# Down projection in halves of 1024 columns, five of 22 pairs of k-tiles by Strassen's seven products

## The chip, the cores and the metric

The kernel runs on one core of a Trainium2 chip. The metric is the device time of one execution in microseconds (us), the median of several runs. The engines have short names in the rows: PE is TensorE's matmul, PEld its load of a stationary operand, DVE is VectorE, ACT is ScalarE, POOL is GpSimd, SP is SyncE, whose queue carries most of the transfers.

## What is computed

One decoder block on 256 tokens (two blocks of 128, called b = 0 and 1) with a model width of 2048:

```python
h = rms_norm(x, w_norm_mix);  proj = h @ w_in          # attention and mLSTM heads follow
x = x + concat([attn_out, mlstm_out]) @ w_out
h2 = rms_norm(x, w_norm_ffn)
x = x + (silu(h2 @ w_ffn_gate) * (h2 @ w_ffn_up)) @ w_ffn_down     # 2048 -> 5632 -> 2048
gate = sigmoid(rms_norm(x, w_norm_ple) @ w_ple_gate)
e = rms_norm(p @ w_ple_proj, w_ple_post_norm)
return x + gate * e
```

All data is float32. The change is in the feed-forward part and its borders: `w_ffn_gate`, `w_ffn_up` and, above all, `w_ffn_down`.

## The kernel before

**How float32 is multiplied.** Each operand is split into a high part rounded to fp32r (a cast on ACT, line 220 for weights) and the rest (a subtraction on DVE, line 221). A product is three matmuls of 128x128 by 128x512: high by high, high by rest, rest by high. `load_piece` (line 212) brings two k-tiles of 512 weight columns (512 KB) into a tile `wr`; `halves` makes `wh` and `wl` of it. `wr`, `wh` and `wl` have four buffers each. A buffer comes free when its last reader is done: `wr` after DVE's subtraction, `wh` and `wl` after the last matmul that reads them.

**The gate and up projection** (`gate_up`, matmuls in lines 742 to 744) runs over eleven chunks of 512 columns. The 16 k-tiles of h2 are taken in eight pairs. A plain pair (`plain_unit`) is two k-tiles by two token blocks by two weights, that is eight products, 24 matmuls. For the pairs 1 and 2 `seven_unit` treats tokens by k-tiles, and k-tiles by (gate, up), as 2 by 2 blocks and takes Strassen's form (Winograd's variant) with seven products, P1 to P7, 21 matmuls. It needs combinations of the weights (tiles `wt`: `t12` and `t34`, four subtractions or additions on DVE in lines 702 to 706, then their halves) and of the tokens (`make_forms`, lines 667 to 678, once per pair: tiles `fh`, `fl`). P1, P5, P6 and P7 have four banks of PSUM of their own, and after the last such pair their sums are formed (lines 749 to 755: `t1`, `qr`, `su`) and later added to the other four banks (lines 757 to 760). A chunk's order is 0, 3, 1, 4, 5, 2, 6, 7 (first chunk: 0, 3, 4, 1, 5, 2, 6, 7): 6 x 24 + 2 x 21 = 186 matmuls.

**The down projection** is `residual(..., "ple")`: four chunks of 512 columns, each one call of `linear` over all 44 k-tiles, 44 x 2 x 3 = 264 matmuls (lines 262 to 264), then two additions to `xres` (line 636) and the task `after`, which transposes the new columns for the next projection: over DRAM by POOL's queue (`split_by_blocks`, lines 187 to 196), and for the last chunk on PE (line 165).

**After it** `e_chunks` multiplies p by `w_ple_proj` (48 matmuls), ACT copies the results out (line 817), and the gate projection runs with 16 pieces of weights per column chunk.

**What sets the order.** Small pieces of work are generators in a list (`Task`); `advance` lets them step between the units of a projection. The tool chain then orders each engine's instructions again by a plan of its own, so that the order on an engine is not that of the code. Engines execute in that order and wait on semaphores.

## Time and profile before

| | |
|---|---|
| median of 3 runs | 1221.85 us (1220.7 to 1222.06) |
| the profiled execution's own time | 1227.3 us |
| its span, from first to last instruction | 1225.1 us |
| PE, DVE, ACT busy in the span | 99%, 70%, 51% |
| mean granted clock of PE | 0.998 of full speed |

The profile is of one execution, which took 5.45 us more than the median. 2.2 us of its time lie outside the span. A busy share counts an instruction from start to end; matmuls overlap each other, so the distance from one start to the next says what a matmul costs, and a wait of a few tenths of a us between two matmuls does not show as idle time.

### The profile page before, as it was taken

The page shows a single profiled execution, that of the slowest core. Times are in us where ns is not written, and L with a number is a line of the kernel's source. Part 1 is how long each engine was busy: PE and PEld are TensorE (multiplying, and loading weights), DVE is VectorE, ACT ScalarE, POOL GpSimd, SP SyncE. Part 2 cuts the span into 40 slices and gives each one's busy share as a digit, 9 for nine tenths or more (in the row PEclk, how much of TensorE's full clock was granted, in tenths as well). Part 3 has the DMA queues.
Part 4 walks back from the last instruction along what each step waited for, and adds up shares of the span by engine and source line. Part 5 has one row for each costly group of instructions (what it writes and reads, how often), then busy time and mean ns, then how long its engine had stood idle before and what let it go on. Part 6 is the DMA issues. An engine that isn't in the chain of part 4 may idle for free. (4 is left out here: it accounts for less than half of the span.)

```text
span 1225.1 us, 15485 instructions
## 1 busy us (share of the span) xinstructions
PE 1211.5 (99%) x5609; PEld 1003.9 (82%) x5609; DVE 854.3 (70%) x1188; ACT 622.8 (51%) x823; POOL 79.5 (6%) x149
## 2 busy tenths in 40 slices
PE   9999999999999999999999999999999999999998
PEld 6899978878888787888788888878888888888888
DVE  5766755565565898888879889888855554545754
ACT  6555556545555545555544555554544444446542
POOL 1111000000011000000000000000000000000000
PEclk9999999999999999999999999999999999999999
DMA  7677744575678667676676776667676666665762
GB/s 262 213 233 221 236 138 131 173 227 157 202 239 254 192 204 232 219 217 210 209 253 194 234 219 216 222 208 251 201 262 206 212 210 210 208 206 170 232 227 92
DMA packets 136384, 257.33 MB, mean 210 GB/s; under 512 B 10002, under 2 KB 29300, under 8 KB 136308
## 3 DMA queue, kind: packets, MB, share of 16 engines
q1 hardware_dynamic: 127156, 229.06, 59.2%
q0 software_dynamic: 8400, 26.22, 6.6%
q8 instruction: 44, 0.72, 0.2%
q10 hardware_dynamic: 752, 1.06, 0.2%
q14 instruction: 32, 0.26, 0.1%
HBM read 241.10 MB, written 15.20 MB: 209 GB/s over the span
## 5 line engine op out<-in xcount | busy, mean ns | idle before, releaser
L221 DVE TENSOR_TENSOR wl<-wr,wh 128x1024 fp32r<-128x1024 f32 (+2 forms) x445 | 508.6, 1154 | 289.4 <-ACT wh L220 288.5
L220 ACT CAST wh<-wr 128x1024 fp32r<-128x1024 f32 (+2 forms) x445 | 439.0, 997 | 449.2 <-PE acc L264 259.1
L262 PE MATMUL acc<-wh,act_h 128*128 128x512 f32 (+2 forms) x864 | 320.6, 371 | 0.1
L263 PE MATMUL acc<-wl,act_h 128*128 128x512 f32 (+2 forms) x864 | 318.0, 368 | 1.6 <-DVE wl L221 1.6
L264 PE MATMUL acc<-wh,act_l 128*128 128x512 f32 (+2 forms) x864 | 317.8, 368 | 0.0
L263 PEld LDWEIGHTS acc<-wl,act_h 128*128 128x128 f32 x864 | 163.0, 189 | 25.8 <-DVE wl L221 2.9
L262 PEld LDWEIGHTS acc<-wh,act_h 128*128 128x128 f32 x864 | 163.1, 189 | 24.6 <-ACT act_h L133 0.9
L264 PEld LDWEIGHTS acc<-wh,act_l 128*128 128x128 f32 x864 | 162.8, 188 | 24.5 <-DVE act_l L135 0.6
L191 POOL DMA_DIRECT2D swap<-tq x100 | 61.0, 616 | 882.1 <-DVE tq L187 882.1
L743 PE MATMUL acc<-wl,act_h 128*128 128x512 f32 x272 | 107.0, 393 | 0.1
L744 PE MATMUL acc<-wh,act_l 128*128 128x512 f32 x272 | 106.0, 390 | 0.0
L742 PE MATMUL acc<-wh,act_h 128*128 128x512 f32 x272 | 103.7, 390 | 0.0
L263 PE MATMUL acc<-wl,gh 128*128 128x512 f32 x224 | 88.3, 394 | 0.0
L262 PE MATMUL acc<-wh,gh 128*128 128x512 f32 x224 | 87.8, 392 | 0.0
L264 PE MATMUL acc<-wh,gl 128*128 128x512 f32 x224 | 86.9, 388 | 0.0
L220 ACT CAST wh<-wt 128x1024 fp32r<-128x1024 f32 x44 | 46.2, 1050 | 55.4 <-DVE wt L703 54.4
L742 PE MATMUL tr<-wh,act_h 128*128 128x512 f32 x178 | 69.5, 391 | 0.2 <-ACT wh L220 0.2
L743 PE MATMUL tr<-wl,act_h 128*128 128x512 f32 x178 | 69.7, 392 | 0.0
L744 PE MATMUL tr<-wh,act_l 128*128 128x512 f32 x178 | 69.3, 389 | 0.0
L743 PEld LDWEIGHTS acc<-wl,act_h 128*128 128x128 f32 x272 | 51.0, 188 | 13.7 <-DVE wl L221 3.3
L742 PEld LDWEIGHTS acc<-wh,act_h 128*128 128x128 f32 x272 | 51.1, 188 | 11.0
L744 PEld LDWEIGHTS acc<-wh,act_l 128*128 128x128 f32 x272 | 51.1, 188 | 10.4
(259 smaller groups left out, 1328.2 us busy)
## 6 DMA issues: line engine op xcount, KB each, us to landing
wr<-in_w_ffn_gate_dram SPq DMA_DIRECT2D x88, 512.0 KB, 3.5
wr<-in_w_ffn_up_dram SPq DMA_DIRECT2D x88, 512.0 KB, 4.5
wr<-in_w_ffn_down_dram SPq DMA_DIRECT2D x88, 512.0 KB, 4.6
wr<-in_w_in_dram SPq DMA_DIRECT2D x63, 512.0 KB, 4.7
wr<-in_w_in_dram SPq DMA_DIRECT2D x48, 344.0 KB, 3.7
wr<-in_w_out_dram SPq DMA_DIRECT2D x32, 512.0 KB, 4.3
wr<-in_w_ple_gate_dram SPq DMA_DIRECT2D x32, 512.0 KB, 4.6
swap<-tq POOLq DMA_DIRECT2D x100, 128.0 KB, 3.6
```

Source lines behind the costliest of these rows:

```text
L191: nc.gpsimd.dma_start(out=d[:, :, :, i, :].rearrange("j c b e -> c b j e"), in_=t[32 * i:32 * i + 32].rearrange("c b j k r -> c b j (k r)"))
L220: nc.scalar.copy(wh, wr)
L221: nc.vector.tensor_tensor(wl, wr, wh.bitcast(F32), op=ALU.subtract)
L262: nc.tensor.matmul(po[b][:, 0:n], ah[:, kk, s], wh[:, j, :], start=count == 1, stop=False)
L263: nc.tensor.matmul(po[b][:, 0:n], ah[:, kk, s], wl[:, j, :], start=False, stop=False)
L264: nc.tensor.matmul(po[b][:, 0:n], al[:, kk, s], wh[:, j, :], start=False, stop=count == total)
L742: nc.tensor.matmul(bank[n], lh, rh, start=first, stop=False)
L743: nc.tensor.matmul(bank[n], lh, rl, start=False, stop=False)
L744: nc.tensor.matmul(bank[n], ll, rh, start=False, stop=left[n] == 0)
```

## The change

The down projection runs in two halves of 1024 columns. In each half the 22 pairs of k-tiles go by a written order; the pairs 8, 10, 12, 14 and 16 take the seven products, with the two blocks of 512 columns in the place of gate and up. A half uses all eight banks of PSUM, so that its sums and additions come once for 1024 columns. The four seven-product sums are added to `xres` apart from the other four banks.

In the gate and up projection `seven_unit` makes the halves in another order and takes P2 as second product, the sums are written in the code behind the halves of the unit that follows, and the sigmoid's tile is `qr` instead of a tile of its own. Around them: columns 1024 to 1535 are transposed on PE too (`after` with c == 2); p is loaded by POOL's queue instead of SP's; the weight row of the last norm is loaded in two transfers of 1024 columns instead of four of 512; `sq` has one buffer instead of two; `rows_b` lies in another pool; `after_up` steps with a gap of 3.

```diff
     def sumsq(dst, src):
-        sq = small.tile([P, 512], BF16, name="sq")
+        sq = small.tile([P, 512], BF16, name="sq", bufs=1)
...
-                if c == 3 and name == "ple":
+                if c >= 2 and name == "ple":
...
                 if c == 3:
+                    while not made_by[id(nxt[2][0])].done:
+                        yield held
...
-                po = linear(w, acts, c * 512, 512, pieces=pieces, width=1 if pieces else 2)
-                for b in range(2):
-                    nc.vector.tensor_tensor(xres[:, b, cs], po[b], xres[:, b, cs], op=ALU.add)
+                if half is None:
+                    po = linear(w, acts, c * 512, 512)
+                    for b in range(2):
+                        nc.vector.tensor_tensor(xres[:, b, cs], po[b], xres[:, b, cs], op=ALU.add)
+                elif c % 2 == 0:
+                    half(c // 2)
...
         def after_up(dst, gg):
-            yield from split_by_blocks(dst, lambda b: gg[b])
+            yield from split_by_blocks(dst, lambda b: gg[b], gap=3)
...
             ra, rb = (load_piece(w, 2 * p, 2, c * 512, 512) for w in (w_gate, w_up))
+            ah, al = halves(ra)
             t12 = fp.tile([P, 2, 512], F32, name="wt", bufs=2)
             nc.vector.tensor_tensor(t12[:, 0], ra[:, 0], rb[:, 0], op=ALU.subtract)
             nc.vector.tensor_tensor(t12[:, 1], t12[:, 0], rb[:, 1], op=ALU.add)
+            h12, l12 = halves(t12)
             t34 = fp.tile([P, 2, 512], F32, name="wt", bufs=2)
             nc.vector.tensor_tensor(t34[:, 0], t12[:, 1], ra[:, 0], op=ALU.subtract)
             nc.vector.tensor_tensor(t34[:, 1], ra[:, 1], t12[:, 1], op=ALU.subtract)
-            ah, al = halves(ra)
-            h12, l12 = halves(t12)
+            h34, l34 = halves(t34)
             bh, bl = halves(rb[:, 1:2])
-            h34, l34 = halves(t34)
-            right = {"P1": (ah[:, 0], al[:, 0]), "P6": (h12[:, 1], l12[:, 1]), "P5": (h12[:, 0], l12[:, 0]),
-                     "P2": (ah[:, 1], al[:, 1]), "P7": (h34[:, 0], l34[:, 0]), "P4": (h34[:, 1], l34[:, 1]),
+            right = {"P1": (ah[:, 0], al[:, 0]), "P2": (ah[:, 1], al[:, 1]), "P6": (h12[:, 1], l12[:, 1]),
+                     "P5": (h12[:, 0], l12[:, 0]), "P7": (h34[:, 0], l34[:, 0]), "P4": (h34[:, 1], l34[:, 1]),
                      "P3": (bh[:, 0], bl[:, 0])}
...
+                if su is None and left["P1"] == 0:
+                    while held:
+                        advance(1)
+                    t1 = fp.tile([P, 512], F32, name="t1")
+                    nc.scalar.copy(t1, bank["P1"])
+                    qr = quads.tile([P, 2, 512], F32, name="quad")
+                    nc.vector.tensor_tensor(qr[:, 0], bank["P6"], t1, op=ALU.add)
+                    nc.vector.tensor_tensor(qr[:, 1], bank["P7"], qr[:, 0], op=ALU.add)
+                    su = quads.tile([P, 2, 512], F32, name="tq")
+                    for i in range(2):
+                        nc.vector.tensor_tensor(su[:, i], bank["P5"], qr[:, i], op=ALU.add)
                 for n, (lh, ll), (rh, rl) in unit:
...
                     nc.tensor.matmul(bank[n], ll, rh, start=False, stop=left[n] == 0)
-                if su is None and left["P1"] == 0:
...
-                sg = fp.tile([P, 512], F32, name="sg", bufs=2)
+                sg = qr[:, b]
...
-        def load_p():
-            yield
-            yield
-            p_sb = fp.tile([P, 512], F32, name="gg0").rearrange("p (b k) -> p b k", b=2)
-            nc.sync.dma_start(out=p_sb, in_=p.rearrange("(b p) k -> p b k", p=P))
-            for _ in range(6):
-                yield
-            yield from transpose_in(acts_p, lambda b, j: p_sb[:, b, j * P:(j + 1) * P], 0, 2)
-        made_by[id(acts_p[0])] = Task(load_p())
...
-                wpost = fp.tile([P, 512], F32, name="sg", bufs=2)
-                nc.sync.dma_start(out=wpost, in_=w_ple_post[0, cs].partition_broadcast(P))
+                if c % 2 == 0:
+                    wpost = fp.tile([P, 1024], F32, name="wt", bufs=2)
+                    nc.sync.dma_start(out=wpost, in_=w_ple_post[0, c * 512:c * 512 + 1024].partition_broadcast(P))
...
-        order = [(k, 2) for k in list(range(16, 4 * NG, 2)) + list(range(0, 16, 2))]
-        acts_h3, rstd3 = residual(w_down, acts_g, v_ple, "ple", pieces=order)
+        seven = (8, 10, 12, 14, 16)
+        orders = ((9, 11, 13, 15, 17, 18, 19, 8, 0, 1, 10, 2, 3, 12, 20, 21, 14, 4, 5, 16, 6, 7),
+                  (9, 11, 8, 13, 15, 17, 10, 18, 19, 0, 12, 1, 2, 3, 14, 4, 5, 16, 20, 21, 6, 7))
...
+        def load_p():
+            p_sb = fp.tile([P, 512], F32, name="gg0").rearrange("p (b k) -> p b k", b=2)
+            nc.gpsimd.dma_start(out=p_sb, in_=p.rearrange("(b p) k -> p b k", p=P))
+            return p_sb
+        def transpose_p(p_sb):
+            t = fp.tile([P, 2, 2, 256], F32R, name="wt", bufs=2)
+            acts_p.extend(t[:, i] for i in range(2))
+            yield from transpose_in(acts_p, lambda b, j: p_sb[:, b, j * P:(j + 1) * P], 0, 2, bank="acc0")
+        def add_seven(c, t1, qr, su):
+            for dst, v in ((xres[:, 0, c:c + 512], t1), (xres[:, 1, c:c + 512], qr[:, 1]),
+                           (xres[:, 0, c + 512:c + 1024], su[:, 0]), (xres[:, 1, c + 512:c + 1024], su[:, 1])):
+                yield
+                nc.vector.tensor_tensor(dst, dst, v, op=ALU.add)
+            held.pop()
...
+        def down_half(c):
+            own, shared = (("acc0", "acc1"), ("tr", "sc"))[::2 * c - 1]
+            tags = {"P1": own[0], "P6": own[0], "P7": own[1], "P5": own[1],
+                    "P2": shared[0], "P3": shared[1], "P4": shared[0], "P8": shared[1]}
+            n7, n8 = len(seven), 2 * (len(orders[c]) - len(seven))
+            left = {"P1": n7, "P6": n7, "P7": n7, "P5": n7, "P8": n8, "P2": n7 + n8, "P3": n7 + n8, "P4": n7 + n8}
+            bank, done = {}, False
+            if c:
+                p_sb = load_p()
+            c1, c2 = slice(c * 1024, c * 1024 + 512), slice(c * 1024 + 512, (c + 1) * 1024)
+            if c == 0:
+                late = new_act()
+                for i, q in enumerate(seven):
+                    if i < 3:
+                        dst = [fp.tile([P, 4, P], F32R, name=f"f{n}{(1, 2, 4)[i]}") for n in "hl"]
+                    else:
+                        dst = [t.rearrange("p k (a b) -> p (k a) b", a=2)[:, 4 * (i - 3):4 * (i - 2)] for t in late]
+                    Task(make_forms(q, *dst), [made_by[id(acts_g[q // 2][0])]])
+            for q in orders[c]:
+                advance(1)
+                if q in seven:
+                    while q not in forms:
+                        advance(1)
+                    unit = seven_unit(c * 1024, q)
+                else:
+                    unit = plain_unit(c * 1024, q)
+                    h = acts_g[q // 2][0]
+                    while not made_by[id(h)].done:
+                        advance(2)
+                advance(1)
+                if not done and left["P1"] == 0:
+                    done = True
+                    while held:
+                        advance(1)
+                    t1 = fp.tile([P, 512], F32, name="t1")
+                    nc.scalar.copy(t1, bank["P1"])
+                    qr = quads.tile([P, 2, 512], F32, name="quad")
+                    nc.vector.tensor_tensor(qr[:, 0], bank["P6"], t1, op=ALU.add)
+                    nc.vector.tensor_tensor(qr[:, 1], bank["P7"], qr[:, 0], op=ALU.add)
+                    su = quads.tile([P, 2, 512], F32, name="tq")
+                    for i in range(2):
+                        nc.vector.tensor_tensor(su[:, i], bank["P5"], qr[:, i], op=ALU.add)
+                    held.append(su)
+                    sums = Task(add_seven(c * 1024, t1, qr, su))
+                    if c:
+                        Task(transpose_p(p_sb), [sums])
+                for n, (lh, ll), (rh, rl) in unit:
+                    first = n not in bank
+                    if first:
+                        bank[n] = ps.tile([P, 512], F32, name=tags[n])
+                    left[n] -= 1
+                    nc.tensor.matmul(bank[n], lh, rh, start=first, stop=False)
+                    nc.tensor.matmul(bank[n], lh, rl, start=False, stop=False)
+                    nc.tensor.matmul(bank[n], ll, rh, start=False, stop=left[n] == 0)
+            while not sums.done:
+                advance(1)
+            for n, b, cs in (("P2", 0, c1), ("P4", 1, c1), ("P3", 0, c2), ("P8", 1, c2)):
+                nc.vector.tensor_tensor(xres[:, b, cs], bank[n], xres[:, b, cs], op=ALU.add)
+        acts_h3, rstd3 = residual(w_down, acts_g, v_ple, "ple", half=down_half)
```

The down projection's own `make_forms`, `plain_unit` and `seven_unit` (left out above) are those of the gate and up projection with `w_down` and two column blocks for the two weights. Each `make_forms` is six DVE instructions and one on ACT, for five pairs.

The second seven-product pair of a gate and up chunk on DVE, and the start of the sums. Before (`wl` from `wr` 128x1024 are halves of a plain unit or of `ra`; from `wt` those of `t12`, `t34`; 128x512 those of `rb`):

```order
L702 TENSOR_TENSOR wt<-wr 128x512
L703 TENSOR_TENSOR wt<-wt,wr 128x512
L221 TENSOR_TENSOR wl<-wr,wh 128x1024
L705 TENSOR_TENSOR wt<-wt,wr 128x512
L706 TENSOR_TENSOR wt<-wr,wt 128x512
L221 TENSOR_TENSOR wl<-wt,wh 128x1024
L221 TENSOR_TENSOR wl<-wr,wh 128x512
L221 TENSOR_TENSOR wl<-wt,wh 128x1024
L751 TENSOR_TENSOR quad<-tr,sg 128x512
L755 TENSOR_TENSOR tq<-sc,quad 128x512
L752 TENSOR_TENSOR quad<-sc,quad 128x512
L221 TENSOR_TENSOR wl<-wr,wh 128x1024
```

Now:

```order
L707 TENSOR_TENSOR wt<-wr 128x512
L708 TENSOR_TENSOR wt<-wt,wr 128x512
L219 TENSOR_TENSOR wl<-wr,wh 128x1024
L711 TENSOR_TENSOR wt<-wt,wr 128x512
L219 TENSOR_TENSOR wl<-wt,wh 128x1024
L712 TENSOR_TENSOR wt<-wr,wt 128x512
L219 TENSOR_TENSOR wl<-wt,wh 128x1024
L219 TENSOR_TENSOR wl<-wr,wh 128x512
L747 TENSOR_TENSOR quad<-tr,t_4403 128x512
L219 TENSOR_TENSOR wl<-wr,wh 128x1024 x2
L748 TENSOR_TENSOR quad<-sc,quad 128x512
L751 TENSOR_TENSOR tq<-sc,quad 128x512 x2
```

The halves of `ra` and `t12` now stand ahead of the second combination of weights, the half of `rb` behind both, and one of four sums instead of three stands ahead of the first halves of the unit behind.

DVE in the down projection, at the first column chunk before (halves of plain pieces, the sums into `xres`, transposes):

```order
L221 TENSOR_TENSOR wl<-wr,wh 128x1024 x9
L130 TENSOR_TENSOR wt<-tr,wt 128x512
L221 TENSOR_TENSOR wl<-wr,wh 128x1024 x6
L636 TENSOR_TENSOR xres<-acc_7697,xres 128x512
L636 TENSOR_TENSOR xres<-acc_7698,xres 128x512
L187 STREAM_TRANSPOSE tq<-xres 128x512 x2
L221 TENSOR_TENSOR wl<-wr,wh 128x1024 x6
L135 SCALAR_TENSOR_TENSOR act_l<-quad,vec_b,act_h 128x256 x4
L221 TENSOR_TENSOR wl<-wr,wh 128x1024 x16
```

The last seven-product pair of the first half now, between plain pieces, up to the second sum:

```order
L219 TENSOR_TENSOR wl<-wr,wh 128x1024 x4
L864 TENSOR_TENSOR wt<-wr 128x512
L865 TENSOR_TENSOR wt<-wt,wr 128x512
L868 TENSOR_TENSOR wt<-wt,wr 128x512
L219 TENSOR_TENSOR wl<-wr,wh 128x1024
L219 TENSOR_TENSOR wl<-wt,wh 128x1024
L869 TENSOR_TENSOR wt<-wr,wt 128x512
L219 TENSOR_TENSOR wl<-wt,wh 128x1024
L219 TENSOR_TENSOR wl<-wr,wh 128x512
L935 TENSOR_TENSOR quad<-tr,t_8535 128x512
L219 TENSOR_TENSOR wl<-wr,wh 128x1024 x2
L936 TENSOR_TENSOR quad<-sc,quad 128x512
```

Four combinations and three and a half splits stand now where two splits stood, and sums stand between the halves of the next units.

PE behind the down projection: `tr<-ident,xres` are transposes, `acc` the products with p. The last of the transposes before:

```order
L165 MATMUL tr<-ident,xres 128x128 x3
L263 MATMUL acc_9395<-wl,wt 128x512
L264 MATMUL acc_9395<-wh,wt 128x512
L262 MATMUL acc_9394<-wh,wt 128x512
L263 MATMUL acc_9394<-wl,wt 128x512
L264 MATMUL acc_9394<-wh,wt 128x512
L262 MATMUL acc_9395<-wh,wt 128x512
L263 MATMUL acc_9395<-wl,wt 128x512
L264 MATMUL acc_9395<-wh,wt 128x512
L165 MATMUL tr<-ident,xres 128x128 x4
L262 MATMUL acc_9426<-wh,wt 128x512
```

And now:

```order
L163 MATMUL tr<-ident,xres 128x128 x3
L262 MATMUL acc_9544<-wh,wt 128x512
L260 MATMUL acc_9545<-wh,wt 128x512
L261 MATMUL acc_9545<-wl,wt 128x512
L262 MATMUL acc_9545<-wh,wt 128x512
L260 MATMUL acc_9544<-wh,wt 128x512
L261 MATMUL acc_9544<-wl,wt 128x512
L262 MATMUL acc_9544<-wh,wt 128x512
L260 MATMUL acc_9545<-wh,wt 128x512
L261 MATMUL acc_9545<-wl,wt 128x512
L262 MATMUL acc_9545<-wh,wt 128x512
L163 MATMUL tr<-ident,xres 128x128 x8
```

Sixteen transposes stand among the products with p, in runs of up to eight, where eight stood.

## Rows read from the trace of the kernel before

**Rows 1.** The page: busy time by engine, and PE's clock in 40 slices.
```profile
PE 1211.5 (99%) x5609; PEld 1003.9 (82%) x5609; DVE 854.3 (70%) x1188; ACT 622.8 (51%) x823; POOL 79.5 (6%) x149
...
PEclk9999999999999999999999999999999999999999
```

**Rows 2.** Busy time by stretch in the down projection: us of each engine (instructions).
```profile
937.00:992.00 55.00, 55.00 (x242) 45.25 (x241) 28.33 (x28) 24.08 (x29) 2.99 (x5) 1.00 0.67 211
```

**Rows 3.** The same, nine stretches of one gate and up chunk each.
```profile
479.90:523.00 43.10, 42.96 (x188) 34.71 (x188) 37.26 (x45) 22.41 (x26) 2.98 (x5) 1.00 0.69 220
...
824.60:867.90 43.30, 43.14 (x188) 34.59 (x187) 37.25 (x45) 22.48 (x26) 2.98 (x5) 1.00 0.69 218
sum 388.00, PE 386.57 PEld 311.59 DVE 334.58 ACT 202.97 POOL 26.91; mean PE 42.95 PEld 34.62 DVE 37.18 ACT 22.55 POOL 2.99
```

**Rows 4.** Timeline of PE in a second seven-product pair: start, duration.
```profile
561.34 0.39 PE L744 MATMUL tr<-wh,act_l 128*128 128x512 f32 x1
561.57 0.40 PE L742 MATMUL tr<-wh,fh 128*128 128x512 f32 x1
562.06 0.50 PE L743 MATMUL tr<-wl,fh 128*128 128x512 f32 x1
562.40 0.39 PE L744 MATMUL tr<-wh,fl 128*128 128x512 f32 x1
562.63 0.39 PE L742 MATMUL sc<-wh,fh 128*128 128x512 f32 x1
...
566.10 0.40 PE L742 MATMUL acc<-wh,act_h 128*128 128x512 f32 x1
```

**Rows 5.** Waits from 500 to 860 us: total us, times, longest.
```profile
ACT wh L220 <- DMA wr<-in_w_ffn_up_dram: 26.4, 20, 3.8
```

**Rows 6.** Waits from 882 to 1118 us, the down projection.
```profile
ACT wh L220 <- PE acc L264: 122.2, 73, 1.7
DVE wl L221 <- ACT wh L220: 109.8, 76, 2.6
```

**Rows 7.** Timeline of DVE beside the pair of rows 4.
```profile
558.45 1.22 DVE L221 TENSOR_TENSOR wl<-wr,wh 128x1024 fp32r<-128x1024 f32 x1
559.59 0.68 DVE L705 TENSOR_TENSOR wt<-wt,wr 128x512 f32<-128x512 f32 x1
560.19 0.68 DVE L706 TENSOR_TENSOR wt<-wr,wt 128x512 f32<-128x512 f32 x1
560.79 1.22 DVE L221 TENSOR_TENSOR wl<-wt,wh 128x1024 fp32r<-128x1024 f32 x1
```

**Rows 8.** Timeline of ACT ahead of that pair.
```profile
547.28 3.14 ACT L220 CAST wh<-wr 128x1024 fp32r<-128x1024 f32 x3 [1.07 <-PE sc L744]
553.70 1.05 ACT L220 CAST wh<-wr 128x1024 fp32r<-128x1024 f32 x1 [3.27 <-DMA wr<-in_w_ffn_up_dram]
```

**Rows 9.** Timeline of SP's queue there: start of each issue.
```profile
546.38 0.37 SPq L212 DMA_DIRECT2D wr<-in_w_ffn_up_dram  x1
```

**Rows 10.** The chain that ended last, in order of time: transposes behind the down projection.
```profile
1121.39 0.35 PE tr L165 x3
...
1123.59 0.44 PE tr L165 x4
```

**Rows 11.** Groups by line on DVE, 400 to 460 us: busy us, mean ns.
```profile
L667 DVE TENSOR_TENSOR tq<-act_h,act_l 128x512 f32<-128x512 f32 x2 | 1.4, 684 | 0.0
...
L672 DVE SCALAR_TENSOR_TENSOR quad<-tq 128x128 f32<-128x128 f32 x2 | 0.6, 288 | 0.0
```

**Rows 12.** Timeline of ACT behind the down projection.
```profile
1121.30 0.63 ACT L116 ACTIVATE sq<-xres 128x512 bf16<-128x512 f32 x1
...
1121.92 0.82 ACT L133 ACTIVATE act_h<-tr,vec_b 128x256 fp32r<-128x256 f32 x2
...
1123.25 1.07 ACT L817 COPY act_h<-acc 128x512 f32<-128x512 f32 x2
```

**Rows 13.** The page: issues of loads, KB each, median us to landing.
```profile
wr<-in_w_ffn_up_dram SPq DMA_DIRECT2D x88, 512.0 KB, 4.5
```

More of the change, by code (lines that the diff above doesn't have):

```diff
@@ L58, in load_x @@
         nc.sync.dma_start(out=xres[:, :, c0:c1], in_=x_v[:, :, c0:c1])
-    rows_b = const.tile([82, P], F32, name="rows_b")
     def load_rows_b():
@@ L309, in block_kernel @@
         tasks = {}
+        rows_b = mp.tile([82, P], F32, name="rows_b")
         def params():
@@ L720, in gate_up @@
                     "P2": shared[0], "P3": shared[1], "P4": shared[0], "P8": shared[1]}
[L721 to L723 removed]
+            order = later_order if c else first_order
+            n7 = len(seven)
+            left = {**{n: n7 for n in ("P1", "P6", "P7", "P5")}, **{n: 16 - n7 for n in ("P2", "P3", "P4")}, "P8": 16 - 2 * n7}
             bank, t1, qr, su = {}, None, None, None
@@ new lines, in plain_unit @@
+        def plain_unit(c, p):
+            w2 = [halves(load_piece(w_down, 2 * p, 2, c + i * 512, 512)) for i in range(2)]
+            h, l = acts_g[p // 2]
+            out = []
+            for j in range(2):
+                k = 2 * (p % 2) + j
+                for b in range(2):
+                    t = slice(b * P, (b + 1) * P)
+                    for i in range(2):
+                        out.append((("P2", "P3", "P4", "P8")[2 * b + i], (h[:, k, t], l[:, k, t]),
+                                    (w2[i][0][:, j, :], w2[i][1][:, j, :])))
+            return out
@@ new lines, in seven_unit @@
+        def seven_unit(c, p):
+            ra, rb = (load_piece(w_down, 2 * p, 2, c + i * 512, 512) for i in range(2))
+            ah, al = halves(ra)
+            t12 = fp.tile([P, 2, 512], F32, name="wt", bufs=2)
+            nc.vector.tensor_tensor(t12[:, 0], ra[:, 0], rb[:, 0], op=ALU.subtract)
+            nc.vector.tensor_tensor(t12[:, 1], t12[:, 0], rb[:, 1], op=ALU.add)
+            h12, l12 = halves(t12)
+            t34 = fp.tile([P, 2, 512], F32, name="wt", bufs=2)
+            nc.vector.tensor_tensor(t34[:, 0], t12[:, 1], ra[:, 0], op=ALU.subtract)
+            nc.vector.tensor_tensor(t34[:, 1], ra[:, 1], t12[:, 1], op=ALU.subtract)
+            h34, l34 = halves(t34)
+            bh, bl = halves(rb[:, 1:2])
+            right = {"P1": (ah[:, 0], al[:, 0]), "P2": (ah[:, 1], al[:, 1]), "P6": (h12[:, 1], l12[:, 1]),
+                     "P5": (h12[:, 0], l12[:, 0]), "P7": (h34[:, 0], l34[:, 0]), "P4": (h34[:, 1], l34[:, 1]),
+                     "P3": (bh[:, 0], bl[:, 0])}
+            return [(n, forms[p][n], v) for n, v in right.items()]
```

60 lines of the change are left out of this document (36 added, 24 removed).

## The prediction

> **What bounds the kernel now.** I read the page first: PE is busy 99% of the span at the full granted clock, DVE 70%, ACT 51% [rows 1]. The reader is to see that nearly all time is a row of matmuls, so that a change can win only by fewer matmuls or by closing small gaps between them. Then the table of stretches, for what a matmul costs: 242 of them fill 55.00 us of the down projection, 0.2273 us each [rows 2]. The list of waits of that stage shows no wait of PE: ACT waits for PE (122.2 us in 73 waits), DVE for ACT (109.8 us) [rows 6]. Both stand at buffers of `wh` and `wl` that PE has yet to free, so DVE, busy 28.33 of 55 us [rows 2], has room.
>
> The gate and up projection is not so smooth. Nine chunks take 388.00 us, 43.11 each [rows 3], and 186 matmuls at 0.2273 would be 42.28: 0.83 too much per chunk. The timeline shows where. Within a seven-product pair the starts are 0.2313 apart (15 in 566.10 - 562.63) [rows 4], which for 42 matmuls is 0.17. The rest, 0.66 per chunk, is waiting. At 561.57 the first matmul of P6 starts, the second, which reads the split of `t12`, 0.49 later and the next 0.34 later [rows 4]: 0.37 lost. DVE began that split only at 560.79 [rows 7], because it came late to the whole pair. Before it ACT had idled 3.27 us for a load of `w_up` that it got at 553.70 [rows 8] and that had been issued at 546.38 [rows 9]. That is 7.3 us where the median is 4.5 [rows 13]; such waits end 20 times in 360 us [rows 5].
>
> **The change, part by part.** Durations are distances between starts: a split of 1024 on DVE 1.14 us, a 512-column combination 0.60 [rows 7], a cast on ACT 1.05 [rows 8].
>
> *Matmuls removed.* Ten seven-product pairs (five in each half) take 21 instead of 24: 30 fewer, 30 x 0.2273 = -6.82 us. The Trainium skill's page "TensorE: Matmul & The Clock Gate", section "Back-to-back issue gap", gives about 131 ns per matmul for a sustained stream of loads and matmuls with 512 columns. By that figure the removal would be an estimated 30 x 0.131 = 3.9 us. This trace does not agree: it has 227 ns in rows 2.
>
> *Matmuls that become dearer.* 210 matmuls stand in seven-product pairs now; with the 0.004 us more of such a pair [rows 2, 4] that is +0.84.
>
> *Transposes moved to PE.* Columns 1024 to 1535 add eight, at 0.44 / 4 = 0.11 [rows 10]: +0.88. PE has no gap to hide them in.
>
> *Work added on DVE and ACT in the down projection.* A plain pair costs DVE 2 x 1.14 = 2.28 us while PE takes 24 x 0.2273 = 5.46. A seven-product pair costs 3 x 1.14 + 0.60 + 4 x 0.60 = 6.42 while PE takes 21 x 0.2313 = 4.86. Over both halves 34 x 2.28 + 10 x 6.42 = 142 us; five forms at 2 x 0.68 + 4 x 0.29 = 2.5 [rows 11] add 13, the sums and additions (2 x 12 at 0.60) 14: 169 of about 234 us, 72%. On average it fits. Locally, let T be the start of a seven-product pair. All four `wh` buffers go to it; two came free a plain pair earlier (5.46 us), in which DVE does 4 x 0.60 + 2 x 1.14 = 4.7. At T the other two come free: `t34` is cast at T + 1.05, split at T + 2.2, needed at T + 3.0 (13 matmuls). The half of `rb` follows at T + 2.8. The first buffer is free again after P1 and P2 (T + 1.4), so the next plain unit's first piece is cast at T + 2.7 and split at T + 3.95, needed at T + 5.1; the second at T + 5.1, needed at T + 5.8. The slack is 0.7 us. The last such pair of a half has one sum (0.60) in front of these splits: 0.1 left. So the pairs should wait for nothing; I take +0.5 for all. The bounds are 0 and the 0.33 that each pair waits now in the gate and up stage (0.66 / 2), 3.3 for ten.
>
> *The forms* are due one after another from the eighth unit on, 7 x 24 x 0.2273 = 38 us into the stage. Their 13 us lie in DVE's room. If that were gone, the first pair would wait by what is missing, within the 3.3.
>
> *Sums and additions at the ends of halves.* The first half's own banks are free before the second starts. The second half ends with four additions; two wait only for banks done 2.0 and 1.4 us before the last matmul, and the transposes that need the last one stand behind twelve matmuls. Behind them, ACT must copy the first product with p out before the third can start, 24 x 0.2273 + 16 x 0.11 = 7.2 us after the end. In front of the copies it now has three squares at 0.63, four `act_h` at 0.41, two casts at 1.05, and the copies are 1.07 [rows 8, 12]: 6.7 us, part of it before the end. Cost nothing; without that cover the four `act_h` that are new ahead of the third, 1.6 us.
>
> *Loads moved.* p's load leaves SP's queue for POOL's, ahead of the second half's swaps, and is due some 100 us later. The second weight row of the last norm waits on SP for the last product with p and holds back the pieces behind it; five gate pieces are issued ahead of it, 5 x 12 x 0.2273 = 13.6 us of matmuls, against 4.5 for a load [rows 13]. Nothing. `sq` with one buffer is written and read by ACT alone, `rows_b` is only placed elsewhere, and the sigmoid's tile `qr` is free by then: nothing, or tenths either way.
>
> *Gate and up.* P6 becomes third product, 0.69 later, and its split stands one combination (0.60) earlier: the 0.37 of rows 4 should go, ten chunks -3.7. Against it, the half of `rb` is now split one full split later (1.14 us), and with it the buffer for the late load of rows 9 comes free later. If the delay passes on, the load's split ends at 553.70 + 1.05 + 1.14 + 1.14 = 557.0. PE's unit began 24 x 0.2273 before the pair at 560.89 (three matmuls ahead of 561.57), at 555.43, and wants that split four matmuls later, at 556.3: 0.7 lost. The load was queued behind other traffic, so I let half of the delay pass: 0.17 lost, +1.7 for ten. Net -2.0; the bounds are -6.6 (all waits go) and +8.3 (0.75 in each of eleven chunks).
>
> *Sum:* -6.82 + 0.84 + 0.88 + 0.5 - 2.0 = -6.6. The profiled execution's 1227.3 would become 1220.7 (span 1225.1 to 1218.5). The median of the runs is 5.45 below the profiled one, and nothing in the change touches that difference: 1221.85 - 6.6 = 1215.3.
>
> **The rivals.**
>
> *A. All waits of the gate and up stage go* (-6.6 instead of -2.0): 1210.7. For it: the new order frees the first buffer after two products (P1, P2) instead of four (P1, P6, P5, P2). Against it: the late load stays. Chance 0.15.
>
> *B. The gate and up stage pays what the down projection wins:* 0.4 per chunk, 4.6 in eleven, cancels the down stage's 6.82 - 0.84 - 0.88 - 0.5 = 4.6: 1221.9. For it: DVE is busy 37.2 of 43.1 us there [rows 3], so lateness is slow to be made good. Chance 0.13.
>
> *C. Slower: the late load.* The place is the second load of the unit behind a chunk's first seven-product pair. Its buffer comes free 1.14 us later, and each us beyond the 0.4 of slack stops PE. In full it costs 0.75 x 11 = 8.3: 1221.85 - 4.6 + 8.3 = 1225.5. It decides from 0.42 per chunk on; at 0.64 the kernel is slower by 0.2%. For it: ACT already waits for that load [rows 8]. Against it: 7.3 us for a load is not set by its issue alone. Chance 0.09.
>
> *D. A removed matmul is worth less than 0.2273*, because the pairs' own waits take part of it: at the bound 3.3 for the ten pairs instead of 0.5 the time is 1218.1. This is in the range of the forecast. By the figure of the Trainium skill's page "TensorE: Matmul & The Clock Gate" the removal would be 2.9 us smaller, an estimated 1218.2. Chance 0.05 for a result set by that.
>
> **How the numbers follow.** The forecast itself (1212.5 to 1218.5) has 0.58. A measurement of this kernel tells about 0.2% (2.4 us) from no change. Faster by more: forecast, A and D, 0.78. Within: B, 0.13. Slower: C, 0.09. The range reaches from A to B: 1210.5 to 1221.8 leaves out C and half of B on one side and a little of A on the other.
>
> **What would show it.** In the profile after: about 30 fewer matmuls and eight more transposes; about 227 ns per matmul in plain stretches of the down projection, 231 in its pairs, and no wait of PE above a few tenths; DVE near 70% there; nine gate and up chunks in about 386 us. More than 388 there, with ACT's waits for `w_up` grown, is B or C; under 384 is A. Waits of PE for splits of `wt` or behind the sums in the down projection would make its own sum wrong, and a stop behind the down projection the free end.

## The result, and the profile after

The changed kernel takes 1229.79 us (median of 5 runs, 1227.57 to 1231.70) against 1222.06 for the kernel before: ratio 1.0053, 95% interval 1.0039 to 1.0067, so 6.5 us slower (4.8 to 8.2; the two medians are 7.7 apart). The forecast was 1215.3 us with a range up to 1221.8, and it gave slower a chance of 0.09. Size and sign were wrong.

The two profiled executions differ by only 1.2 us (1228.54, span 1226.8, against 1227.3), because that of before lies more than 5 us above its own median. Of this, 4.4 us lie ahead of the change: its gate and up stage begins at 403.47 us, that of the changed kernel at 399.06. So I compare stages.

The page of the changed kernel, busy time by engine, answers to [rows 1]:
```profile
PE 1208.7 (99%) x5587; PEld 997.2 (81%) x5587; DVE 917.3 (75%) x1292; ACT 638.6 (52%) x850; POOL 77.5 (6%) x145
```
PE has 22 instructions fewer, as it should (30 matmuls fewer, eight transposes more), but is busy only 2.8 us less. The stretches of the changed kernel, cut at the first matmul of the gate and up stage, of the down projection and of what follows (columns as in [rows 2]):
```profile
399.06:878.48 479.42, 474.23 (x2047) 381.14 (x2046) 415.33 (x508) 246.14 (x282) 33.01 (x55) 1.00 0.68 218
878.48:1120.79 242.31, 238.52 (x1031) 191.68 (x1030) 183.69 (x224) 118.39 (x138) 9.75 (x16) 1.00 0.62 208
1120.79:1226.80 106.01, 101.28 (x545) 87.73 (x543) 64.69 (x98) 53.62 (x82) 0.00 (x0) 0.99 0.54 177
```
and the first two of the kernel before, cut in the same way:
```profile
403.47:878.79 475.32, 472.49 (x2047) 380.93 (x2046) 410.56 (x506) 248.06 (x280) 32.90 (x55) 1.00 0.69 218
878.79:1120.15 241.36, 241.36 (x1062) 198.67 (x1061) 127.78 (x127) 104.41 (x118) 11.97 (x20) 1.00 0.67 215
```
Gate and up takes 4.1 us more where I forecast 2.0 less. The down projection takes 1.0 more where I forecast 5.5 less: before, PE was busy there for all of 241.36 us, and now it stands idle for 3.8 of 242.31 (242.31 - 238.52), beside smaller stops that still count as busy. The nine chunks of [rows 3] sum to 389.57 now:
```profile
sum 389.57, PE 387.03 PEld 312.15 DVE 336.33 ACT 199.99 POOL 27.01; mean PE 43.00 PEld 34.68 DVE 37.37 ACT 22.22 POOL 3.00
```
Waits from 880 to 1120 us in the changed kernel (the stage of [rows 6], where no wait of PE was found):
```profile
DVE wl L219 <- ACT wh L218: 33.3, 26, 3.1
...
DVE wt L864 <- DMA wr<-in_w_ffn_down_dram: 14.9, 8, 4.0
...
PEld sc L950 <- DVE wl L219: 4.8, 6, 1.8
PEld acc L950 <- DVE wl L219: 4.6, 9, 1.1
...
PE sc L950 <- DVE wl L219: 2.6, 4, 1.4
```
PE now waits for splits on DVE. DVE waits for casts on ACT and, ahead of its first combination (L864), for a load.

To see which units wait I took the starts of all matmuls of these two stages. Each distance from one to the next above 0.26 us counts, less 0.228, as a wait. Sums in us (chunks counted from 0, one execution for each column):
```
gate and up, chunks 1 to 10        before  changed    e2     e3     e4    e10
first pair and the unit behind       3.44     0.00   0.00   2.23   0.00   0.00
second pair                          2.13     3.67   2.35   0.72   2.69   1.26
unit behind the second pair          0.54     7.04   6.91   1.81   8.39   4.87
all units                            6.93    11.99   9.26   4.94  11.42   6.21

down projection                   changed    e3    e6    e7    e8   e10   e11   e12
1st half, first pair, unit behind    2.37  1.12  2.50  1.93  0.00  2.36  3.99  2.15
1st half, four other pairs, same     3.17  3.68  0.85  0.00  3.23  0.00  0.00  0.00
second half                          2.31  1.91  2.55  1.28  2.87  2.34  0.94  1.36
all units                            8.13  6.70  5.90  3.19  6.09  4.69  5.00  3.51
```
Three things limit this table. The second half's row holds 0.36 in each column that is no wait: four transposes of p stand between two matmuls there. In e11, 1.6 of the 3.99 are matmuls at the lower clock (the last section). And executions scatter: the eight kernels whose gate and up stage is that of e3 have 4.3 to 5.8 in its last row, and e12, whose stage is that of e10, has 9.63, with 2.81 of it ahead of the second pair.

The forecast had 0.5 where 7.8 stands (8.13 without the transposes). In gate and up the waits at P6, which stands third now, went as forecast: 4.55 in the ten chunks (2.42 in the first pairs, all 2.13 in the second) became 0. Larger ones came up at P7 of the second pair (3.67) and in the unit behind it (0.54 to 7.04).

DVE at the second pair of chunk 7, changed kernel:
```profile
731.92 0.69 DVE L712 TENSOR_TENSOR wt<-wr,wt 128x512 f32<-128x512 f32 x1
733.80 1.23 DVE L219 TENSOR_TENSOR wl<-wt,wh 128x1024 fp32r<-128x1024 f32 x1 [1.19 <-ACT wh L218]
734.94 0.69 DVE L219 TENSOR_TENSOR wl<-wr,wh 128x512 fp32r<-128x512 f32 x1
735.54 0.69 DVE L747 TENSOR_TENSOR quad<-tr,t 128x512 f32<-128x512 f32 x1
736.15 2.35 DVE L219 TENSOR_TENSOR wl<-wr,wh 128x1024 fp32r<-128x1024 f32 x2
```
and ACT beside it:
```profile
732.72 1.05 ACT L218 CAST wh<-wt 128x1024 fp32r<-128x1024 f32 x1 [2.43 <-DVE wt L712]
733.67 0.62 ACT L218 CAST wh<-wr 128x512 fp32r<-128x512 f32 x1
```
L712 makes the second half of `t34`. DVE's next instruction is the split of `t34`, which needs ACT's cast of it, so DVE idles 1.19 us. The half of `rb`, whose raw data had long been there, stands behind on both queues: its cast follows that of `t34` on ACT, and its split that of `t34` on DVE. Then come a sum and the next unit's two splits, which begin at 736.15 and 737.29. PE wants the second of them at 738.22 (0.23 after 737.99) and gets it at 738.55:
```profile
737.76 0.39 PE L759 MATMUL acc<-wh,act_l 128*128 128x512 f32 x1
737.99 0.40 PE L757 MATMUL acc<-wh,act_h 128*128 128x512 f32 x1
738.55 0.50 PE L758 MATMUL acc<-wl,act_h 128*128 128x512 f32 x1 [0.17 <-DVE wl L219]
738.89 0.39 PE L759 MATMUL acc<-wh,act_l 128*128 128x512 f32 x1
```
DVE at the last pair of the first down half, whose matmuls begin at 983.56:
```profile
980.39 0.69 DVE L864 TENSOR_TENSOR wt<-wr 128x512 f32<-128x512 f32 x1 [3.06 <-DMA wr<-in_w_ffn_down_dram]
981.12 0.69 DVE L865 TENSOR_TENSOR wt<-wt,wr 128x512 f32<-128x512 f32 x1
981.84 0.69 DVE L868 TENSOR_TENSOR wt<-wt,wr 128x512 f32<-128x512 f32 x1
982.45 1.22 DVE L219 TENSOR_TENSOR wl<-wr,wh 128x1024 fp32r<-128x1024 f32 x1
983.59 1.22 DVE L219 TENSOR_TENSOR wl<-wt,wh 128x1024 fp32r<-128x1024 f32 x1
984.72 0.69 DVE L869 TENSOR_TENSOR wt<-wr,wt 128x512 f32<-128x512 f32 x1
986.60 1.23 DVE L219 TENSOR_TENSOR wl<-wt,wh 128x1024 fp32r<-128x1024 f32 x1 [1.19 <-ACT wh L218]
```
Here the chain is late from its start: the second raw piece lands 3.2 us before the pair begins, and from the first combination on, four combinations, two splits, the idle time for the cast and the split of `t34` take 7.4 us.

### The profile page after: what moved, and what is told of

Read it like the earlier page. It is cut to its first block, busy times and chain, and to the rows that moved or that the text cites. A ratio compares the mean times of both kernels' runs of the same rounds, so it can differ in the third digit from the quotient of the medians.

```text
span 1226.8 us, 15607 instructions
## 1 busy us (share of the span) xinstructions
PE 1208.7 (99%) x5587; PEld 997.2 (81%) x5587; DVE 917.3 (75%) x1292; ACT 638.6 (52%) x850; POOL 77.5 (6%) x145
## 4 chain that ended last, share of the span: by engine, by line
PE 57%; DVE 20%; DMA 12%; issue 6%; ACT 4%; POOL 1%; SPq 0%; DVEq 0%; ACTq 0%; POOLq 0%
DVE wl L219 10%; PE acc L261 9%; PE acc L262 9%; PE acc L260 9%; PE acc L758 3%; PE acc L759 3%; PE acc L757 3%; ACT wh L218 3%; DMA wr<-in_w_ffn_up_dram 3%; DMA wr<-in_w_ffn_down_dram 3%; DMA quad<-swap 2%; DMA swap<-tq 2%; DMA wr<-in_w_in_dram 2%; PE sc L758 1%; PE sc L759 1%
## 5 line engine op out<-in xcount | busy, mean ns | idle before, releaser
L260 PE MATMUL acc<-wh,act_h 128*128 128x512 f32 (+2 forms) x736 | 270.2, 367 | 0.4 <-ACT act_h L131 0.4
L261 PE MATMUL acc<-wl,act_h 128*128 128x512 f32 (+2 forms) x736 | 267.4, 363 | 1.1 <-DVE wl L219 1.1
L262 PE MATMUL acc<-wh,act_l 128*128 128x512 f32 (+2 forms) x736 | 267.6, 364 | 0.0
L261 PEld LDWEIGHTS acc<-wl,act_h 128*128 128x128 f32 x736 | 138.7, 188 | 19.8 <-DVE wl L219 1.9
L260 PEld LDWEIGHTS acc<-wh,act_h 128*128 128x128 f32 x736 | 138.7, 188 | 19.6 <-ACT act_h L131 0.9
L262 PEld LDWEIGHTS acc<-wh,act_l 128*128 128x128 f32 x736 | 138.5, 188 | 19.3 <-DVE act_l L133 0.6
L218 ACT CAST wh<-wt 128x1024 fp32r<-128x1024 f32 x64 | 67.1, 1049 | 116.8 <-DVE wt L708 55.6
L219 DVE TENSOR_TENSOR wl<-wt,wh 128x1024 fp32r<-128x1024 f32 x64 | 78.1, 1221 | 23.3 <-ACT wh L218 22.6
L758 PEld LDWEIGHTS acc<-wl,act_h 128*128 128x128 f32 x272 | 51.0, 188 | 16.5 <-DVE wl L219 6.2
L757 PEld LDWEIGHTS acc<-wh,act_h 128*128 128x128 f32 x272 | 51.1, 188 | 11.1 <-ACT wh L218 0.4
L759 PEld LDWEIGHTS acc<-wh,act_l 128*128 128x128 f32 x272 | 51.1, 188 | 10.3
L758 PE MATMUL sc<-wl,act_h 128*128 128x512 f32 x144 | 56.7, 394 | 0.9 <-DVE wl L219 0.9
L759 PE MATMUL sc<-wh,act_l 128*128 128x512 f32 x144 | 56.1, 389 | 0.0
```

Source lines behind the costliest of these rows:

```text
L218: nc.scalar.copy(wh, wr)
L219: nc.vector.tensor_tensor(wl, wr, wh.bitcast(F32), op=ALU.subtract)
L260: nc.tensor.matmul(po[b][:, 0:n], ah[:, kk, s], wh[:, j, :], start=count == 1, stop=False)
L261: nc.tensor.matmul(po[b][:, 0:n], ah[:, kk, s], wl[:, j, :], start=False, stop=False)
L262: nc.tensor.matmul(po[b][:, 0:n], al[:, kk, s], wh[:, j, :], start=False, stop=count == total)
L757: nc.tensor.matmul(bank[n], lh, rh, start=first, stop=False)
```

## The experiments

Each kernel was timed against the kernel before on the same chip, but not all on one chip, so that two rows are compared by their ratios and not by their medians. "us" is (ratio - 1) x 1222.
```
                         median   ratio   95% interval        us
changed kernel          1229.79  1.0053  1.0039 to 1.0067   +6.5
e1_down_alone           1224.94  1.0020  1.0009 to 1.0030   +2.4
e2_gate_up_alone        1225.98  1.0026  1.0012 to 1.0039   +3.2
e3_old_halves           1224.06  1.0009  0.9995 to 1.0022   +1.1
e4_old_sums             1233.09  1.0074  1.0053 to 1.0095   +9.0
e5_down_plain           1223.40  0.9997  0.9986 to 1.0008   -0.4
e6_down_old_order       1224.13  0.9991  0.9980 to 1.0002   -1.1
e7_own_rb               1218.69  0.9962  0.9948 to 0.9976   -4.6
e8_no_forms             1220.91  0.9972  0.9959 to 0.9984   -3.4
e9_first_pair_later     1224.53  1.0010  0.9996 to 1.0024   +1.2
e10_t34_last            1220.07  0.9976  0.9961 to 0.9991   -2.9
e11_rb_and_t34          1219.04  0.9956  0.9939 to 0.9972   -5.4
e12_all_t34             1220.62  0.9970  0.9953 to 0.9988   -3.7
e13_pool_forms          1227.93  1.0028  1.0014 to 1.0042   +3.4
```

### Which stage, and what in gate and up

**e1_down_alone**: gate and up's `seven_unit` as before, the block of sums behind the matmuls again, `gap=2`.

> The changed kernel with the gate and up stage written as before (order of combinations, splits and products, sums right behind the pair's matmuls, gap 2). Theory 'two stages': the profile of the changed kernel has the gate and up stage 4.1 us longer than before (479.4 against 475.3) and the down projection 1.0 longer (242.3 against 241.4), so the median falls by 4.1 to about 1225.7, and the down projection stays near 242.3. Rival 'down only': the gate and up stage differs only by chance from one execution to another; the median stays at 1229.8.

+2.4 instead of +6.5: the stage as before gives 4.1 back. The down projection stays long (242.7 us).

**e2_gate_up_alone**: the kernel before with only that stage changed.

> The kernel before with the gate and up stage of the changed kernel alone. Theory 'two stages': 1222.1 + 4.1 = 1226.2, with PE waiting in the unit behind each chunk's second seven-product pair. Rival 'down only': 1222.1. The forecast's term of -2.0 for this stage: 1220.1.

+3.2, and the table shows its waits behind the second pair (6.91). Both stages are at fault (2.4 + 3.2 against 6.5). The forecast's -2.0 is refuted, and so is the rival.

**e3_old_halves**: the changed kernel with this put back in gate and up:
```diff
-            ah, al = halves(ra)
             t12 = ...
-            h12, l12 = halves(t12)
             t34 = ...
-            h34, l34 = halves(t34)
+            ah, al = halves(ra)
+            h12, l12 = halves(t12)
             bh, bl = halves(rb[:, 1:2])
-            right = {P1, P2, P6, P5, P7, P4, P3}
+            h34, l34 = halves(t34)
+            right = {P1, P6, P5, P2, P7, P4, P3}
```


> The changed kernel with only the order of combinations, splits and products in the gate and up stage put back; the sums stay behind the next unit's halves. Theory 'order of the splits' (the split of t34 stands right behind its combination, so VectorE idles 1.19 us for ScalarE's cast and everything behind it is late): the stage gets back all of its 4.1 us, 1225.7. Rival 'place of the sums' (the sum written ahead of the next unit's matmuls takes 0.6 us of VectorE in front of that unit's splits): stays at 1229.8.

+1.1, and the units behind the second pairs wait 1.81 in sum instead of 7.04. In chunk 7 the idle time before the split of `t34` is shorter, though P7, the first product that reads it, is fifth as before:
```profile
733.22 1.23 DVE L219 TENSOR_TENSOR wl<-wt,wh 128x1024 fp32r<-128x1024 f32 x1 [0.41 <-ACT wh L218]
```
The order is the cause, not the place of the sums.

**e4_old_sums**: the other half of the edit put back, the block of sums behind the matmuls.

> The changed kernel with only the sums of the gate and up stage put back, right behind the pair's matmuls; the new order of splits and products stays. Theory 'order of the splits': no better than 1228.8. Rival 'place of the sums': about 1225.7, and the unit behind the second seven-product pair waits for nothing.

+9.0, no better than the changed kernel: with the sums back in their old place the waits behind the second pair are still 8.39, so the rival falls. Whether the new place is worth anything is not shown. The intervals of the two kernels overlap, all ten chunks' waits are about the same (11.42 and 11.99), and the profiled execution of e4 took 1226.23 us, 6.9 less than its median.

**e10_t34_last**: the changed kernel, and in both stages
```diff
-            h34, l34 = halves(t34)
             bh, bl = halves(rb[:, 1:2])
+            h34, l34 = halves(t34)
-            right = {P1, P2, P6, P5, P7, P4, P3}
+            right = {P1, P2, P6, P5, P3, P7, P4}
```


> The changed kernel, with one thing changed in both stages: the half of rb is split ahead of t34, and P3 stands ahead of P7 and P4 (P1, P2, P6, P5, P3, P7, P4). Theory 'VectorE idles for t34's cast, and what stands behind it is late': the split of rb fills half of the 1.19 us, and P7 needs t34 0.68 later. In the gate and up stage the waits behind the second pair (0.7 a chunk, 7.0 in ten) and in it (3.7) mostly go, in the down projection 2 to 3 of 8.1: 8 to 12 less than the changed kernel, level with before or up to 4 below. Rival 'the products' (P2 second, so that P6, P5, P7 all stand later and buffers come free in another order): 6.5 above before as the changed kernel, within 2.

-2.9, 9.4 us better than the changed kernel by moving the half of `rb` and its product ahead. P2 is still second, so the rival falls. The edit does two things that this run does not tell apart: it shortens the idle time, and it lets P7 need `t34` three matmuls later. e3 has the first without the second. DVE's second pair of chunk 7 in this kernel:
```profile
726.41 0.69 DVE L712 TENSOR_TENSOR wt<-wr,wt 128x512 f32<-128x512 f32 x1
727.10 0.69 DVE L219 TENSOR_TENSOR wl<-wr,wh 128x512 fp32r<-128x512 f32 x1
728.29 1.22 DVE L219 TENSOR_TENSOR wl<-wt,wh 128x1024 fp32r<-128x1024 f32 x1 [0.50 <-ACT wh L218]
```
The idle time is 0.50 instead of 1.19. In six of ten chunks the unit behind still waits 0.6 to 0.8 us, so the cure of this stage is not complete.

### What makes the down projection late

These start from e3_old_halves (+1.1).

**e5_down_plain**: `seven = ()`, and without pairs no forms and no sums.

> As e3_old_halves, but the down projection in halves of 1024 columns with no seven-product pair: 1056 matmuls, no forms, no sums. Theory 'the pairs': the halves themselves cost nothing, so the down projection takes 1056 x 0.2273 + 0.44 = 240.5 us without a wait of PE, about what it takes in e3_old_halves with 30 matmuls fewer (241.0), and the median stays within 1 us of that kernel's 1224. Rival 'the structure' (eight banks, 88 loads in another order, four additions at a half's end): waits of several us stay and the median is 4 to 7 us higher, since the 30 matmuls come back and the waits stay.

-0.4; the down projection takes 241.34 us with 0.1 us of waits. Halves, banks and loads cost nothing. In e3_old_halves it takes 241.02: ten pairs with 30 matmuls fewer give back nearly all that they save.

**e6_down_old_order**: the pairs of the down projection, too, in the order of the `+` lines of e3.

> As e3_old_halves, but the seven-product pairs of the down projection too with all four combinations ahead of the splits and the half of rb split ahead of t34 (the order that the gate and up stage had before). Theory 'order of the splits': VectorE no longer idles for the cast of t34, the waits at the 13th and 14th matmul of a pair and in the unit behind (about 5 us of the 7 us of waits in the down projection) mostly go; -3, about 1221. Rival 'late raw loads' (four raw buffers, so that the second raw piece of a pair lands only 4 us before the pair begins): the order changes little, 1224 +- 1.

-1.1, 2.2 better than e3_old_halves, with overlapping intervals: by time alone this is inconclusive. By the table the waits at the four later pairs fall by 2.8 us and those at the first one rise by 1.4.

**e7_own_rb**:
```diff
-            ra, rb = (load_piece(w_down, 2 * p, 2, c + i * 512, 512) for i in range(2))
+            ra = load_piece(w_down, 2 * p, 2, c, 512)
+            rb = fp.tile([P, 2, 512], F32, name="rb")
+            nc.sync.dma_start(out=rb, in_=w_down[...])
```
and one more `new_act()` holds the forms that lay where `rb` is now.

> As e3_old_halves, but the second raw piece of a down pair has a buffer of its own, so that the ring of four loses two places to a pair only once. Theory 'late raw loads': VectorE's waits for loads ahead of the first combination (14.9 us in 8 in the changed kernel) fall below 5, the down projection loses 2 to 4 us, median about 1221. Rival 'order of the splits': these waits fall, but PE's waits behind t34's cast stay; 1223 to 1224.

-4.6, 5.7 better than e3_old_halves; the down projection takes 237.15 us, and the later pairs of the first half wait for nothing. Where I was wrong: DVE's waits for loads did not fall (17.7 us in 8), since DVE now comes to them earlier. What counts is the distance to the pair. The last pair of the first half begins at 976.70, and DVE's first combination for it is 6.7 us ahead, not 3.2:
```profile
969.96 0.69 DVE L866 TENSOR_TENSOR wt<-wr,rb 128x512 f32<-128x512 f32 x1 [1.18 <-DMA wr<-in_w_ffn_down_dram]
```
SP's own waits name the buffer. From 880 to 1120 us in the changed kernel:
```profile
SPq L210 <- DVE wl L219: 155.8, 78, 6.7
SPq L210 <- DVE wt L869: 38.7, 6, 7.7
```
and in e7_own_rb:
```profile
SPq L210 <- DVE wl L219: 142.6, 75, 6.4
SPq L863 <- DVE wl L219: 38.9, 9, 5.3
...
SPq L210 <- DVE wt L871: 4.9, 1, 4.9
```
In the changed kernel loads wait 38.7 us for a pair's last combination (L869), the last reader of its first raw piece. In e7_own_rb SP still waits 38.9 us, but for the buffer of `rb`, and its waits in these rows sum to 186.4 instead of 194.5 us: the wait has moved more than it has shrunk. How a late pair delays the next one shows between the fourth and the fifth pair of the changed kernel's first half:
```profile
969.30 1.23 DVE L219 TENSOR_TENSOR wl<-wt,wh 128x1024 fp32r<-128x1024 f32 x1 [1.19 <-ACT wh L218]
970.44 4.09 DVE L219 TENSOR_TENSOR wl<-wr,wh 128x512 fp32r<-128x512 f32 x4
...
973.42 6.87 DMA wr<-in_w_ffn_down_dram
```
Behind the idle time for the fourth pair's `t34` come four splits without a pause. The third of them ends at 973.41 and frees a raw buffer, and the load of the fifth pair's second raw piece starts at 973.42 and lands at 980.29, the 3.2 us ahead of that pair. That is a loop, and the first half's waits grow along it (0.23, 0.56, 1.45 at the third, fourth and fifth pair). e10_t34_last, with the buffers of the changed kernel, loosens it too: its first combination for the last pair stands 4.4 us ahead of that pair (972.22 to 976.57).

**e8_no_forms**: `make_forms` sets `forms[p]` from `h` and `l` alone, so that the kernel leaves out the sums of tokens.

> As e3_old_halves, but the five forms of the down projection are left out: all seven products of a pair read the plain activations instead (the output lacks the sums of Strassen's left factors). Theory 'forms in front of the first pair's last split': the first pair of the first half and the unit behind it (2.4 us of waits) run through, nothing else changes; 1221.7. Rival: the first pair is late for the same reason as the others, and waits 0.5 us or more without the forms; 1223.5 or more.

-3.4; the first pair and the unit behind it wait for nothing, as the theory says (e6 and e7, which have the forms, wait 2.50 and 1.93 there). But e3_old_halves lost only 1.12 there in its profiled execution, and the time fell by 4.5 us. That difference stays open.

**e9_first_pair_later**: based on e7_own_rb; first half `(9, 11, 13, 15, 17, 18, 19, 0, 8, 1, 2, 10, 3, 20, 12, 21, 4, 14, 5, 6, 16, 7)`.

> As e7_own_rb, with another order of units in the first half: the first seven-product pair stands one plain pair later, two plain pairs between all pairs, one behind the last. In e7_own_rb the first pair waits 1.22 us and the unit behind it 0.71, since VectorE is still at the five forms. Theory 'forms': one plain pair more gives VectorE 5.46 - 2.28 = 3.2 us of room, more than the 2.4 us of forms that stand between this pair's splits; both waits go, -1.9 from e7_own_rb (median some 4.6 below before), so about 6.5 below before. Rival: the first pair's splits are late because of their own order, and wait the same wherever the pair stands; as e7_own_rb, 4.6 below before.

+1.2: wrong both ways. The compiled order of instructions moved the forms along with the pair, and ACT's queue stood 4.03 us until DVE had made the last form, with the cast of the pair's `t34` behind it:
```profile
920.32 0.62 ACT L838 CAST act_h<-quad 128x512 fp32r<-128x512 f32 x1 [4.03 <-DVE quad L836]
920.85 1.04 ACT L218 CAST wh<-wt 128x1024 fp32r<-128x1024 f32 x1
```
And with one plain pair left behind the last pair, sums, additions and transposes of the half (from 987.17 to 997.84 on DVE, with one pair of splits between them) stand in front of the second half's splits: PE waits there 3.01 us.

### The remedies together

**e11_rb_and_t34**: e7_own_rb with e10's two lines in the down projection.

> As e7_own_rb, and in the down projection's pairs the half of rb is split ahead of t34 and P3 stands ahead of P7. In e7_own_rb the down projection still waits 3.2 us, 1.9 of it at the first pair and behind it, 0.8 at the second half's second pair. Theory 'two remedies for the same waits' (late raw load and idle for t34's cast add up to one lateness, and either remedy is enough for the pairs of the first half behind the first): no more than 0.5 to 1 us better than e7_own_rb, 4.6 to 6 below before. Rival 'two separate losses': each remedy takes its own 3 to 4 us, 8 to 9 below before.

**e12_all_t34**: e10_t34_last with e7's buffer.

> The changed kernel with both remedies: t34 last in both stages (as e10_t34_last), and a buffer of its own for the second raw piece of a down pair. e10_t34_last is 3.0 below before and waits 4.7 us in the down projection, 2.4 of it at the first pair. Theory 'two remedies for the same waits': 0.5 to 1.5 better than e10_t34_last, 3.5 to 4.5 below before. Rival 'two separate losses': 6 to 7 below before.

-5.4 and -3.7: each within 1 us of its base (e7_own_rb and e10_t34_last), so late load and idle time are one lateness; what the rival expected (8 to 9 and 6 to 7 below before) lies outside both intervals. Either remedy is enough for the first half's pairs behind the first: these wait for nothing in e7, e10, e11 and e12. All four beat both kernels. e7_own_rb and e11_rb_and_t34 are lowest, 0.4% below before and 11 to 12 us below the changed one.

**e13_pool_forms**: e11_rb_and_t34 with the forms' `nc.vector` made `nc.gpsimd`.

> As e11_rb_and_t34, with the additions that make the five forms on GpSimd instead of VectorE (the same values, with five additions per form for four). Theory 'forms on VectorE make the first pair late': VectorE loses about 11 us of work between 895 and 923 us, the first pair and the unit behind it wait for nothing, 1.5 to 2 below e11_rb_and_t34. Rival 'GpSimd is slow or holds VectorE up': the forms themselves come late, PE waits several us for the forms of the first pair, and the kernel is slower than e11_rb_and_t34. Rival 'own order': the first pair waits 1 us or more although VectorE is free.

+3.4: the second theory of the three. GpSimd's first form becomes late (892.84 to 903.1, with a wait of 4.81 us for a split on DVE in it), and DVE slows beside GpSimd. The first pair and the unit ahead of it lose 11.1 us, 2.6 of it in matmuls at the lower clock. So the forms are what makes the first pair late (e8), but neither a later pair nor GpSimd hides them.

## Why the prediction was wrong

*Matmuls removed, -6.82:* right in number and price: a plain stretch of the second half has 72 in 16.32 us, 0.2267 each. *Dearer in pairs, +0.84:* wrong, close to nothing: a pair that does not wait takes 4.78 us, 21 x 0.2276, as the last two of the second half do. No distance in rows 4's stretch is a wait by the measure above; why a pair's matmuls were 0.2313 apart there stays open.

*Own waits of the ten pairs, +0.5:* 7.8, the largest error, and the step that failed. The upper bound 3.3 was the waits of pairs in another stage; it bounded nothing here. The walk from T let the four combinations be done before T and asked only for `wh` buffers and DVE's time. Two things failed in it. The second raw piece lands 3.2 us before T, because the ring of four raw buffers is held up by the pair before (e7). And the walk put cast and split of `t34` one behind the other without asking what DVE does meanwhile: it stands 1.19 us, and what is queued behind stands with it (e10).

*Forms, "lie in DVE's room":* wrong as to place. On average there is room (DVE is busy 183.69 of 242.31 us, 76%; I said 72), but the forms come in a lump ahead of the first pair: 2.37 us of waits, and none without the forms (e8).

*Transposes, +0.88:* right. From the end of the down projection to PE's last matmul 101.00 us pass (1120.79 to 1221.79) instead of 100.18 (1120.15 to 1220.33). *Ends of halves, loads moved, 0:* right; the first unit of the second half waits for nothing.

*Gate and up, -2.0:* this step failed too. The gain was right in cause and near in size: -3.7 was forecast at P6, and 4.55 went. There was luck in the size, for the 0.37 of one second pair stood for a whole chunk, and a chunk had 0.46 in its two pairs. The loss, +1.7, was put at the wrong pair and given the wrong cause: not the late load behind the first pair (rival C's place), where PE waits for nothing now, but the splits in and behind the second, held up by the idle time for `t34`. The sign that the prediction named for B or C did appear: 389.57 us for the nine chunks, and ACT's waits for `w_up` (rows 5: 26.4 in 20) at
```profile
ACT wh L218 <- DMA wr<-in_w_ffn_up_dram: 36.5, 17, 3.1
```
But e10_t34_last has 30.2 there and little more than half of PE's waits, so the sign does not name the cause. Rival B's price for this stage (+4.6) was near the measured +4.1; it had no place for it, and its time (1221.9) was not near.

The sum with these terms: -6.82 + 0.81 + 7.8 + 5.7 (waits of all eleven chunks, 14.25 against 8.57 us) = +7.5, against 6.5 (4.8 to 8.2). By the lengths of the three stages it is 4.1 + 1.0 + 1.1 = +6.1. The difference is in gate and up, where the distances that count as no wait became 1.6 us shorter in sum; why is not shown.

## What to carry to other kernels

Behind every instruction that waits for another engine's answer, list what stands in the same queue and is ready: moving one split that could be ready, with its cast and its product, ahead of one that waits was worth 9 us here. When a stage gets a unit that holds more buffers for longer, walk the loads as well: from the release of the raw buffer to landing to the first use, around the ring until it repeats. An average share of 76% says nothing about a lump of work with a due time.
